# Weight sums of the seven-for-eight groups by accumulating DMAs instead of VectorE subtractions

## The chip, the cores and the metric

The kernel runs on one core of one Trainium2 chip. The metric is the device time of one execution in microseconds. Before the change it is 3290.38 us, the median of three runs between 3289.5 and 3291.68 us.

## The reference, cut to what matters

The reference is one layer of one model followed by one layer of another, on 256 tokens of width 2048, all in float32. The first layer mixes tokens with a state space branch and a gated delta rule, then has a feed-forward network with a convolution. The second layer has a feed-forward network, a pooling and linear attention mixer, and a second feed-forward network. The change touches only the two feed-forward networks of the second layer:

```python
def swiglu(h, w_in, w_out):          # h: 256 x 2048, D_FF = 5632
    gu = h @ w_in                    # w_in: 2048 x 11264
    gate, up = gu[..., :D_FF], gu[..., D_FF:]
    return (jax.nn.silu(gate) * up) @ w_out

h = h + 0.5 * swiglu(rmsnorm_2(h, ffn1_norm[l]), ffn1_w_in[l], ffn1_w_out[l])
...
h = h + 0.5 * swiglu(rmsnorm_2(h, ffn2_norm[l]), ffn2_w_in[l], ffn2_w_out[l])
```

## The kernel before

Float32 products are made of three reduced-precision products. Each operand is split into a high part (a cast to fp32r) and a low part (the rest). For a weight block of 128x1024, loaded as 512 KB, ScalarE makes the high part (line 126) and VectorE subtracts it to get the low part (line 127), in `split_raw`. TensorE then adds high x high, high x low and low x high into PSUM.

The main stream of a feed-forward network runs through `gemm_tg` (lines 201 to 203): each block feeds 12 matmuls of 512 columns. Its blocks are loaded by `load_w` (line 85) on SP's queue into four `wr` buffers; the high and low parts have three buffers each (`wh`, `wl`).

The 5632 hidden columns are worked in 11 groups of 512, each with a gate half and an up half. Six groups are `plain`. The groups 3, 4, 5, 7 and 9 are made by `seven`. It treats the product as a 2x2 block problem: the 256 tokens are two halves of 128, the 2048 inputs are two halves of 1024, and gate and up are the two halves of the outputs. With sums of activations (made once in `x_sums`, kept in `sx`) and sums of weight blocks it needs seven block products where the plain way needs eight. Each `seven` call has 28 passes: a pass takes one weight block or one weight sum of 128x1024, splits it into `sh` and `sl` (two buffers each) and runs 6 matmuls (lines 1133 to 1135) into one of four PSUM banks `ps[0]` to `ps[3]`.

`together` interleaves the two streams: one step is one pass of `seven` and one block of the main stream (up blocks of a `plain` group or blocks of the down projection `down_g`), so 6 and 12 matmuls. The tile framework sets the order of instructions on each engine from the order in the code and their priority; splits and weight sums are raised with `tc.high_priority(offset=600)`. Semaphores are put in by the framework where a tile is written, read or its buffer reused.

In `seven` before the change, `block` loads a weight block with SP: the first of each chain through `load_w`, the others into three `ws` buffers (line 1142). `less` makes a weight sum as a VectorE subtraction (recorded at the helper's line 368) into one of two `tt` buffers. In the first loop the sums form a chain for each of four `jj`: t1 = b12 - b11, t2 = b22 - t1, t4 = b21 - t2, and the four passes of one `jj` follow each other. In the second loop each `jj` has three passes, one of them on the sum b22 - b12. At the end of a group the banks are added to partial results kept in `w5`, `w6` and `gs`, and gate and up are joined.

Of the kernel before, what the change touches and what calls it, by code (L numbers as in the profile page):

```python
# [11 lines left out]
F32 = mybir.dt.float32  # L12
# [3 lines left out]
ALU = mybir.AluOpType  # L16
PSUM = bass.MemoryType.PSUM

P = 128
# [32 lines left out]
def tile_kernel(ctx: ExitStack, tc: tile.TileContext, A, out):  # L52
    nc = tc.nc
    act, dve, pe, pool_e, sp = nc.scalar, nc.vector, nc.tensor, nc.gpsimd, nc.sync
# [11 lines left out]
    def bank():  # L66
        if side_full[0]:
            return pg.tile([P, 512], F32, tag="pt", name="side2")
        return px.tile([P, 512], F32, tag="side", name="side")

    def v3(ap, b):
        return ap.rearrange("p (a b) -> p a b", b=b)
# [10 lines left out]
    def load_w(src, n=1024):  # L83
        raw = wp.tile([P, n], F32, tag="wr", bufs=4, name="wr")
        sp.dma_start(out=raw, in_=src)
        return raw

    x0, xq0 = [], []
    for q in range(4):
        t = xp.tile([P, 4, T], F32, tag=f"x{q}", name=f"x{q}")  # L90
# [207 lines left out]
    class Norm:  # L298
# [5 lines left out]
        def add(self, q, t, xk):  # L304
            if self.ss is None:
                self.ss = ev2.tile([P, 4, 2], F32, tag="ss", bufs=3, name="ss")
            junk = ev2.tile([P, 512], F32, tag="sq", bufs=1, name="sq")
            act.activation(junk, xk, AF.Square, accum_out=self.ss[:, q, t : t + 1])
            if (q, t) == (2, 1):
                act.activation(warm, self.ss[:, 2, :], AF.Sqrt)  # L310
# [56 lines left out]
    def sub(o, a, b):  # L367
        dve.tensor_tensor(out=o, in0=a, in1=b, op=ALU.subtract)  # L368
# [7 lines left out]
    def stt(o, a, s, b, op0, op1):  # L376
        dve.scalar_tensor_tensor(out=o, in0=a, scalar=s, in1=b, op0=op0, op1=op1)
# [43 lines left out]
    def wsrc(name, b, n=2):  # L421
        return [A[name][n * b + i] for i in range(n)]
# [6 lines left out]
    ps = bank()  # L429
# [11 lines left out]
    first = [gemm_f32(raw0 if b == 0 else [load_w(s) for s in wsrc("w_u", b)], xg) for b in range(nu)]  # L441
# [239 lines left out]
    for hd in range(HEADS):  # L681
        t = mp.tile([P, 2, T], F32, tag=f"qk{hd}", name=f"qk{hd}")
        v = mp.tile([P, T], F32, tag=f"v{hd}", name=f"v{hd}")
        for part, dst in ((0, t[:, 1, :]), (1, t[:, 0, :]), (2, v)):
            b = 3 * hd + part
            if b % 6 == 5:
                ps = gemm_f32([load_w(s) for s in wsrc("w_qkv", b)], x0)
            else:
                ps = gemm(wsrc("w_qkv", b), hs)
# [5 lines left out]
    raw = wp.tile([P, KT * 16], F32, tag="wr", bufs=4, name="wba")  # L695
# [5 lines left out]
    ps = pg.tile([P, T], F32, tag="pt", name="pt")  # L701
# [63 lines left out]
    for m in range(8):  # L765
        ps = gemm(wsrc("w_z", m), hs)
# [248 lines left out]
    for q in range(4):  # L1015
        t = xp.tile([P, 2, 512], F32, tag=f"x{q}", name=f"xt{q}")
# [33 lines left out]
    def ffn(up, down, hs, rstd, conv_w, scale, fin, gain=None, nxt=None, before_last=None):  # L1050
        with tc.tile_pool(name="hid", bufs=2) as hd:
# [48 lines left out]

            sx = []

            def x_sums():
                for j in range(8):
                    f = hd.tile([P, 2, T], F32, tag="g", bufs=1, name="xf")
                    s = hd.tile([P, 4, P], F32, tag="w", bufs=1, name="xs")
                    for i in range(2):
                        add(f[:, i, :], hs[j + 8 * i][:, 0, :].bitcast(F32), hs[j + 8 * i][:, 1, :].bitcast(F32))  # L1110
                    add(s[:, 0, :], f[:, 0, P:], f[:, 1, P:])
                    sub(s[:, 1, :], s[:, 0, :], f[:, 0, :P])
                    sub(s[:, 2, :], f[:, 0, :P], f[:, 0, P:])
                    sub(s[:, 3, :], f[:, 1, :P], s[:, 1, :])
                    e = []
                    for i in range(2):
                        t = hp.tile([P, 2, 2, P], F32R, tag=f"h{j + 8 * i}", name=f"sx{j}_{i}")
                        act.copy(out=t[:, 0], in_=s[:, 2 * i : 2 * i + 2, :])
                        sub(t[:, 1], s[:, 2 * i : 2 * i + 2, :], t[:, 0].bitcast(F32))
                        e += [(t[:, 0, c, :], t[:, 1, c, :]) for c in range(2)]  # L1120
                    sx.append(e)
                    yield

            def seven(g):

                ps = [px.tile([P, 512], F32, tag="side", name="side7") for _ in range(4)]

                def passes(ps, xa, raw, first, last):
                    to = [hd.tile([P, 1024], F32R, tag=n, bufs=2, name=n) for n in ("sh", "sl")]
                    hi, lo = (v3(a, 512) for a in split_raw(raw, to=to))  # L1130
                    for i in range(2):
                        xh, xl = xa(i)
                        pe.matmul(ps, xh, hi[:, i, :], start=first and i == 0, stop=False, skip_group_check=True)  # L1133
                        pe.matmul(ps, xh, lo[:, i, :], start=False, stop=False, skip_group_check=True)  # L1134
                        pe.matmul(ps, xl, hi[:, i, :], start=False, stop=last and i == 1, skip_group_check=True)  # L1135

                def block(k2, half, tag=None):
                    src = A[up][16 * g + 8 * half + k2]
                    if tag is None:
                        return load_w(src)  # L1140
                    raw = hd.tile([P, 1024], F32, tag=tag, bufs=3, name="ws")
                    sp.dma_start(out=raw, in_=src)
                    return raw

                def less(a, b):
                    t = hd.tile([P, 1024], F32, tag="tt", bufs=2, name="tt")
                    with tc.high_priority(offset=600):
                        sub(t, a, b)
                    return t

                def hx(k, t):
                    return lambda i: (hs[k + i][:, 0, P * t : P * t + P], hs[k + i][:, 1, P * t : P * t + P])

                def sxs(j, c):
                    return lambda i: sx[j + i][c]

                gs, w5, w6 = (hd.tile([P, 512], F32, tag=n, bufs=1, name=n) for n in ("g", "w", "w6"))
                for jj in range(4):
                    j, fl = 2 * jj, dict(first=jj == 0, last=jj == 3)
                    b11, b12 = block(jj, 0), block(jj, 1, "ws")  # L1160
                    t1 = less(b12, b11)
                    passes(ps[0], hx(j, 0), b11, **fl)
                    if jj == 3:
                        act.copy(out=w6, in_=ps[0])
                    yield
                    b22 = block(4 + jj, 1, "ws")
                    passes(ps[1], sxs(j, 0), t1, **fl)
                    if jj == 3:
                        add(w5, ps[1], w6)
                    yield  # L1170
                    b21 = block(4 + jj, 0, "ws")
                    t2 = less(b22, t1)
                    passes(ps[2], sxs(j, 1), t2, **fl)
                    if jj == 3:
                        add(gs, ps[2], w6)
                    yield
                    t4 = less(b21, t2)
                    passes(ps[3], hx(8 + j, 1), t4, **fl)
                    if jj == 3:
                        add(w6, ps[3], w6)  # L1180
                    yield
                for jj in range(4):
                    j, fl = 2 * jj, dict(first=False, last=jj == 3)
                    passes(ps[0], hx(8 + j, 0), block(4 + jj, 0, "ws"), **fl)
                    yield
                    b22 = block(4 + jj, 1, "ws")
                    passes(ps[1], sxs(j, 3), b22, **fl)
                    yield
                    passes(ps[2], sxs(j, 2), less(b22, block(jj, 1, "ws")), **fl)
                    yield  # L1190
                rc = late[0]
                t = hd.tile([P, 2, 512], F32, tag="tt", bufs=2, name="gates")
                act.activation(t[:, 0], ps[0], AF.Silu, scale=rc[:, 0:1])
                add(t[:, 1], ps[2], w6)
                act.activation(t[:, 1], t[:, 1], AF.Silu, scale=rc[:, 1:2])
                add(gs, ps[1], gs)
                add(w5, ps[2], w5)
                a = gs, w5
                for i in range(2):
                    stt(a[i], a[i], rc[:, i : i + 1], t[:, i], ALU.mult, ALU.mult)  # L1200
                yield
                new_ys(g)
                return_turn = lambda: turn_hidden(a, ys[g])
                if g == 3:
                    pend.append(return_turn)
                else:
                    after.append(return_turn)
                yield
# [108 lines left out]
    half = cst2[:, P + 5 * T : P + 5 * T + 2]  # L1317
# [162 lines left out]
    for g in range(4):  # L1480
        up = gp_.tile([P, 2, 16 + T], F32, tag="up", bufs=2, name="up")
# [202 lines left out]
```

## Time and profile before

| what | value |
|---|---|
| median of three runs | 3290.38 us |
| the profiled execution, whole program | 3289.64 us |
| its span | 3287.8 us |
| TensorE clock granted in it | 0.999 of full speed |
| busy share: PE, VectorE, ScalarE, GpSimd | 99%, 79%, 54%, 0% |
| read from HBM | 661 MB |

The span is the time from the first to the last instruction of the profiled execution; what the program takes beyond it lies around it. PE is TensorE's matmul side and PEld its weight loads, which overlap. DVE is VectorE, ACT ScalarE, POOL GpSimd, and SP the engine whose queue issues the loads (SPq). L1133 is line 1133 of the kernel. A group of instructions is named by what it writes and reads, `sl<-tt,sh` being the low part of a weight sum. A wait is put down to what released it.

### The profile page before, as it was taken

How to read it: one execution, taken by the hardware profiler on the slowest of the kernel's cores; microseconds unless marked ns; L12 is line 12 of the kernel's file. 1: busy time of each engine (PE TensorE's matmuls, PEld its weight loads, DVE VectorE, ACT ScalarE, POOL GpSimd, SP SyncE). 2: the span in 40 equal slices, each digit the busy share in tenths (PEclk: the TensorE clock that was granted, in tenths of full speed). 3: DMA queues.
4: the chain of work that ended last, by engine and by line, in shares of the span. 5: the costliest groups of instructions: out<-in, count | busy, mean ns of one | idle time of the engine just before them, and what ended most of it. 6: DMA issues, size and time to landing. Idle time of an engine off the chain costs nothing.

```text
span 3287.8 us, 44587 instructions
## 1 busy us (share of the span) xinstructions
PE 3265.2 (99%) x16530; PEld 2742.9 (83%) x16530; DVE 2588.5 (79%) x3758; ACT 1774.7 (54%) x2523; POOL 4.0 (0%) x22
## 2 busy tenths in 40 slices
PE   9999999999999999999999999999999999999998
PEld 8887988888888888888888888888888888888887
DVE  8999987666877767677987887875786988878876
ACT  4566666445555445455655555545555655555554
POOL 0000000000000000000000000000000000000000
PEclk9999999999999999999999999999999999999999
DMA  6445543365555555556777777765545677777774
GB/s 223 156 152 174 179 144 116 108 225 180 192 187 188 190 188 188 188 187 204 255 247 248 246 247 243 246 197 190 173 146 195 229 243 248 249 245 243 247 253 148
DMA packets 186873, 666.09 MB, mean 203 GB/s; under 512 B 20880, under 2 KB 25488, under 8 KB 186272
## 3 DMA queue, kind: packets, MB, share of 16 engines
q1 hardware_dynamic: 186080, 662.21, 61.3%
q8 instruction: 129, 2.11, 0.3%
q10 hardware_dynamic: 576, 1.05, 0.1%
q14 instruction: 88, 0.72, 0.1%
HBM read 661.08 MB, written 2.10 MB: 202 GB/s over the span
## 4 chain that ended last, share of the span: by engine, by line
PE 94%; DVE 4%; issue 1%; ACT 1%; DMA 0%; SPq 0%; DVEq 0%
PE ptt L201 18%; PE ptt L202 18%; PE ptt L203 18%; PE pt L170 13%; PE pt L172 6%; PE side L1134 4%; PE side L1135 4%; PE side L1133 4%; DVE wl L127 1%; PE pt L135 1%; PE pt L137 1%; PE pt L136 1%; PE pt L245 1%; PE side L874 1%; PE side L885 1%; PE side L620 1%
## 5 line engine op out<-in xcount | busy, mean ns | idle before, releaser
L126 ACT CAST wh<-wr 128x1024 fp32r<-128x1024 f32 x937 | 984.2, 1051 | 1221.9 <-PE ptt L203 839.4
L127 DVE TENSOR_TENSOR wl<-wr,wh 128x1024 fp32r<-128x1024 f32 x937 | 1146.1, 1223 | 539.0 <-ACT wh L126 534.2
L170 PE MATMUL pt<-h,wh 128*128 128x512 f32 x1792 | 632.1, 397 | 0.0
L172 PE MATMUL pt<-h,wl 128*128 128x256 f32 x1792 | 502.5, 281 | 0.0
L201 PE MATMUL ptt<-wh,h 128*128 128x512 f32 x1088 | 428.3, 394 | 0.0
L202 PE MATMUL ptt<-wl,h 128*128 128x512 f32 x1088 | 425.5, 391 | 0.0
L203 PE MATMUL ptt<-wh,h 128*128 128x512 f32 x1088 | 424.2, 390 | 0.0
L202 PE MATMUL ptt<-wl,hid 128*128 128x512 f32 x1040 | 409.0, 394 | 0.0
L201 PE MATMUL ptt<-wh,hid 128*128 128x512 f32 x1040 | 408.4, 393 | 0.5 <-ACT wh L126 0.5
L203 PE MATMUL ptt<-wh,hid 128*128 128x512 f32 x1040 | 408.4, 394 | 0.0
L170 PEld LDWEIGHTS pt<-h,wh 128*128 128x128 f32 x1792 | 336.3, 188 | 80.9 <-issue 1.0
L172 PEld LDWEIGHTS pt<-h,wl 128*128 128x128 f32 x1792 | 338.3, 189 | 0.6
L201 PEld LDWEIGHTS ptt<-wh,h 128*128 128x128 f32 x1088 | 204.2, 188 | 46.7 <-ACT wh L126 1.2
L203 PEld LDWEIGHTS ptt<-wh,h 128*128 128x128 f32 x1088 | 204.3, 188 | 44.0 <-issue 0.4
L202 PEld LDWEIGHTS ptt<-wl,h 128*128 128x128 f32 x1088 | 204.2, 188 | 43.4
L201 PEld LDWEIGHTS ptt<-wh,hid 128*128 128x128 f32 x1040 | 195.4, 188 | 45.7 <-ACT wh L126 1.0
L202 PEld LDWEIGHTS ptt<-wl,hid 128*128 128x128 f32 x1040 | 195.6, 188 | 44.1
L203 PEld LDWEIGHTS ptt<-wh,hid 128*128 128x128 f32 x1040 | 195.4, 188 | 43.6 <-DVE hid L368 0.5
L127 DVE TENSOR_TENSOR sl<-tt,sh 128x1024 fp32r<-128x1024 f32 x160 | 195.9, 1224 | 21.9 <-ACT sh L126 21.3
L126 ACT CAST sh<-tt 128x1024 fp32r<-128x1024 f32 x160 | 168.3, 1052 | 52.9 <-PE side L1135 48.1
L135 PE MATMUL pt<-h,wl 128*128 128x256 f32 x512 | 149.5, 292 | 0.0
L137 PE MATMUL pt<-h,wh 128*128 128x256 f32 x512 | 145.3, 284 | 0.0
(420 smaller groups left out, 4957.9 us busy)
## 6 DMA issues: line engine op xcount, KB each, us to landing
wr<-in_f_up SPq DMA_DIRECT2D x408, 512.0 KB, 4.3
wr<-in_f_down SPq DMA_DIRECT2D x265, 512.0 KB, 4.3
ws<-in_f_up SPq DMA_DIRECT2D x240, 512.0 KB, 4.3
wr<-in_w_qkv SPq DMA_DIRECT2D x48, 512.0 KB, 3.3
wr<-in_w_gs SPq DMA_DIRECT2D x32, 512.0 KB, 3.3
wr<-in_w_gd SPq DMA_DIRECT2D x32, 512.0 KB, 3.3
wr<-in_w_glu SPq DMA_DIRECT2D x32, 512.0 KB, 3.3
wr<-in_w_out SPq DMA_DIRECT2D x32, 512.0 KB, 3.3
```

The lines of the kernel that those rows point to most:

```text
L126: act.copy(out=hi, in_=raw)
L127: dve.tensor_tensor(out=lo, in0=raw, in1=hi.bitcast(F32), op=ALU.subtract)
L135: pe.matmul(ps, wl, xt[:, 0, :], start=first, stop=False)
L137: pe.matmul(ps, wh, xt[:, 0, :], start=False, stop=last)
L170: pe.matmul(ps.rearrange("p a b -> p (a b)"), hi[:, j, :], xts[k].rearrange("p a b -> p (a b)"), start=k == 0, stop=False, skip_group_chec ...
L172: pe.matmul(ps[:, 0, :], lo[:, j, :], xts[k][:, 0, :], start=False, stop=k == n - 1, skip_group_check=True)
L201: pe.matmul(pss[t], xh, hi[:, j, :], start=k == 0, stop=False)
L202: pe.matmul(pss[t], xh, lo[:, j, :], start=False, stop=False)
L203: pe.matmul(pss[t], xl, hi[:, j, :], start=False, stop=k == n - 1)
L1133: pe.matmul(ps, xh, hi[:, i, :], start=first and i == 0, stop=False, skip_group_check=True)
L1134: pe.matmul(ps, xh, lo[:, i, :], start=False, stop=False, skip_group_check=True)
L1135: pe.matmul(ps, xl, hi[:, i, :], start=False, stop=last and i == 1, skip_group_check=True)
```

## The change

In `seven` a weight sum is no longer subtracted on VectorE. The first block of a chain is loaded by SP into one of now five `tt` tiles (`base`); after a pass has split that tile, a DMA issued by GpSimd adds the next block onto it in place (`accum_op=ALU.add`), and the next pass of the chain splits the same tile again. Two chains (`pair`) alternate. [...] `block`, `less` and the three `ws` buffers are gone; one block in the second loop is loaded by `load_w`.

```diff
-                    add(s[:, 0, :], f[:, 0, P:], f[:, 1, P:])
-                    sub(s[:, 1, :], s[:, 0, :], f[:, 0, :P])
+                    sub(s[:, 0, :], f[:, 1, P:], f[:, 0, P:])
+                    stt(s[:, 1, :], s[:, 0, :], -1.0, f[:, 0, :P], ALU.mult, ALU.subtract)
                     sub(s[:, 2, :], f[:, 0, :P], f[:, 0, P:])
-                    sub(s[:, 3, :], f[:, 1, :P], s[:, 1, :])
+                    stt(s[:, 3, :], f[:, 1, :P], -1.0, s[:, 1, :], ALU.mult, ALU.subtract)
...
+                def src(k2, half):
+                    return A[up][16 * g + 8 * half + k2]
+
+                def base(k2, half):
+                    t = hd.tile([P, 1024], F32, tag="tt", bufs=5, name="tt")
+                    sp.dma_start(out=t, in_=src(k2, half))
                     return t
...
-                for jj in range(4):
-                    j, fl = 2 * jj, dict(first=jj == 0, last=jj == 3)
-                    b11, b12 = block(jj, 0), block(jj, 1, "ws")
-                    t1 = less(b12, b11)
-                    passes(ps[0], hx(j, 0), b11, **fl)
...
-                    b22 = block(4 + jj, 1, "ws")
-                    passes(ps[1], sxs(j, 0), t1, **fl)
...
-                    b21 = block(4 + jj, 0, "ws")
-                    t2 = less(b22, t1)
-                    passes(ps[2], sxs(j, 1), t2, **fl)
...
-                    t4 = less(b21, t2)
-                    passes(ps[3], hx(8 + j, 1), t4, **fl)
...
+                for pair in ((0, 1), (2, 3)):
+                    tt = {jj: base(jj, 0) for jj in pair}
+                    for n in range(4):
+                        for jj in pair:
+                            xa = (hx(2 * jj, 0), sxs(2 * jj, 0), sxs(2 * jj, 1), hx(8 + 2 * jj, 1))[n]
+                            passes(ps[n], xa, tt[jj], first=jj == 0, last=jj == 3)
+                            if n < 3:
+                                pool_e.dma_start(out=tt[jj], in_=(src(jj, 1), src(4 + jj, 1), src(4 + jj, 0))[n],
+                                                 accum_op=ALU.add)
...
+                            yield
+                for pair in ((0, 1), (2, 3)):
+                    tt = {jj: base(4 + jj, 1) for jj in pair}
+                    for n in (1, 2, 0):
+                        for jj in pair:
+                            xa = (hx(8 + 2 * jj, 0), sxs(2 * jj, 3), sxs(2 * jj, 2))[n]
+                            passes(ps[n], xa, tt[jj] if n else load_w(src(4 + jj, 0)), first=False, last=jj == 3)
+                            if n == 1:
+                                pool_e.dma_start(out=tt[jj], in_=src(jj, 1), accum_op=ALU.add)
+                            yield
...
-                add(gs, ps[1], gs)
-                add(w5, ps[2], w5)
+                stt(gs, gs, -1.0, ps[1], ALU.mult, ALU.subtract)
+                stt(w5, w5, -1.0, ps[2], ALU.mult, ALU.subtract)
```

## Rows read from the trace of the kernel before

**Rows 1.** The page's head and first line of part 1: busy us (share) xinstructions.
```profile
span 3287.8 us, 44587 instructions
...
PE 3265.2 (99%) x16530; PEld 2742.9 (83%) x16530; DVE 2588.5 (79%) x3758; ACT 1774.7 (54%) x2523; POOL 4.0 (0%) x22
```

**Rows 2.** The page's part 4, shares of the chain by engine.
```profile
PE 94%; DVE 4%; issue 1%; ACT 1%; DMA 0%; SPq 0%; DVEq 0%
```

**Rows 3.** Windows: start:end length, busy us (x) per engine, PEclk, DMA share, GB/s.
```profile
1577.70:2213.00 635.30, 635.30 (x2796) 517.62 (x2795) 525.27 (x527) 338.36 (x351) 0.00 (x0) 1.00 0.74 241
2612.00:3213.00 601.00, 601.00 (x2646) 489.68 (x2645) 493.50 (x466) 318.22 (x326) 0.00 (x0) 1.00 0.76 246
```

**Rows 4.** Longest waits of PE, whole run: total us, times, longest us.
```profile
PE side L438 <- DVE sq L365: 6.2, 1, 6.2
PE side L655 <- DVE xa L362: 5.4, 4, 3.6
```

**Rows 5.** Tile `tt`: xcount, ns min/median/max, first and last start in us.
```profile
L368 DVE TENSOR_TENSOR tt<-ws,tt x80: 1217/1225/1236, 1573.3 to 3157.0; 128x1024 f32<-128x1024 f32 x80
L368 DVE TENSOR_TENSOR tt<-ws,wr x40: 1215/1225/1243, 1567.6 to 3144.6; 128x1024 f32<-128x1024 f32 x40
L368 DVE TENSOR_TENSOR tt<-ws x40: 1217/1226/1227, 1634.0 to 3204.3; 128x1024 f32<-128x1024 f32 x40
```

**Rows 6.** Tile `gates`, VectorE at a group's end.
```profile
L365 DVE TENSOR_TENSOR gates<-side,w x10: 683/684/687, 1694.0 to 3223.1; 128x512 f32<-128x512 f32 x10
...
L377 DVE SCALAR_TENSOR_TENSOR g<-g,rc,gates x10: 744/751/754, 1696.4 to 3219.7; 128x512 f32<-128x512 f32 x10
```

**Rows 7.** Longest wait of GpSimd, whole run.
```profile
POOL mean_g L1319 <- PE ptt L203: 2256.9, 1, 2256.9
```

**Rows 8.** Waits of SP's queue, 1569 to 2200 us.
```profile
SPq L1142 <- DVE tt L368: 138.9, 74, 3.2
```

**Rows 9.** DMA issues, 1569 to 2215 us: xcount, KB each, median us to landing.
```profile
ws<-in_f_up SPq DMA_DIRECT2D x117, 512.0 KB, 4.3
wr<-in_f_up SPq DMA_DIRECT2D x101, 512.0 KB, 4.5
```

**Rows 10.** Timeline around 1802 us: start, length in us, instruction [idle before <-releaser].
```profile
1802.84 0.39 PE L1133 MATMUL side<-sh,sx 128*128 128x512 f32 x1
...
1804.44 1.05 ACT L126 CAST sh<-ws 128x1024 fp32r<-128x1024 f32 x1 [0.35 <-PE side L1135]
...
1805.52 1.23 DVE L127 TENSOR_TENSOR sl<-ws,sh 128x1024 fp32r<-128x1024 f32 x1 [0.18 <-ACT sh L126]
...
1811.19 0.39 PE L1133 MATMUL side<-sh,sx 128*128 128x512 f32 x1
```

**Rows 11.** DMA issues, 600 to 800 us.
```profile
wr<-in_w_out SPq DMA_DIRECT2D x32, 512.0 KB, 3.3
...
gb<-in_gain SPq DMA_DIRECT2D x1, 1024.0 KB, 5.5
```

**Rows 12.** DMA packets and issues, 2590 to 2612 us.
```profile
DMA packets 1751, 6.37 MB, mean 290 GB/s; under 512 B 199, under 2 KB 199, under 8 KB 1750
...
wr<-in_f_up SPq DMA_DIRECT2D x9, 512.0 KB, 5.5
ws<-in_f_up SPq DMA_DIRECT2D x5, 512.0 KB, 5.3
```

**Rows 13.** Timeline of PE in a plain stage, first and last of 15 starts.
```profile
2547.79 0.39 PE L203 MATMUL ptt<-wh,yg 128*128 128x512 f32 x1
...
2550.97 0.39 PE L202 MATMUL ptt<-wl,yg 128*128 128x512 f32 x1
```

**Rows 14.** Tile `side`, the first matmul line of a pass.
```profile
L1133 PE MATMUL side<-sh,sx x320: 393/394/483, 1581.9 to 3221.4; 128*128 128x512 f32 x160
...
L1133 PE MATMUL side<-sh,h x240: 393/394/483, 1577.7 to 3213.0; 128*128 128x512 f32 x120
```

More of the change, by code (lines that the diff above doesn't have):

```diff
@@ L1135, in passes @@
                         pe.matmul(ps, xl, hi[:, i, :], start=False, stop=last and i == 1, skip_group_check=True)
[L1137 to L1148, printed above, removed]
+                def src(k2, half):
[3 more added lines that the diff above has]
+                    sp.dma_start(out=t, in_=src(k2, half))
                     return t
@@ L1157, in seven @@
                 gs, w5, w6 = (hd.tile([P, 512], F32, tag=n, bufs=1, name=n) for n in ("g", "w", "w6"))
-                for jj in range(4):
-                    j, fl = 2 * jj, dict(first=jj == 0, last=jj == 3)
-                    b11, b12 = block(jj, 0), block(jj, 1, "ws")
-                    t1 = less(b12, b11)
-                    passes(ps[0], hx(j, 0), b11, **fl)
-                    if jj == 3:
-                        act.copy(out=w6, in_=ps[0])
-                    yield
-                    b22 = block(4 + jj, 1, "ws")
-                    passes(ps[1], sxs(j, 0), t1, **fl)
-                    if jj == 3:
-                        add(w5, ps[1], w6)
-                    yield
-                    b21 = block(4 + jj, 0, "ws")
-                    t2 = less(b22, t1)
-                    passes(ps[2], sxs(j, 1), t2, **fl)
-                    if jj == 3:
-                        add(gs, ps[2], w6)
-                    yield
-                    t4 = less(b21, t2)
-                    passes(ps[3], hx(8 + j, 1), t4, **fl)
-                    if jj == 3:
-                        add(w6, ps[3], w6)
-                    yield
@@ L1182, in seven @@
[L1182 to L1190, printed above, removed]
+                for pair in ((0, 1), (2, 3)):
[7 more added lines that the diff above has]
+                                                 accum_op=ALU.add)
+                            if jj == 3 and n == 0:
+                                act.copy(out=w6, in_=ps[0])
+                            elif jj == 3:
+                                add((w5, gs, w6)[n - 1], ps[n], w6)
+                            yield
@@ L1191, in seven @@
                 rc = late[0]
-                t = hd.tile([P, 2, 512], F32, tag="tt", bufs=2, name="gates")
+                t = hd.tile([P, 2, 512], F32, tag="tt", bufs=5, name="gates")
                 act.activation(t[:, 0], ps[0], AF.Silu, scale=rc[:, 0:1])
```

## The prediction

> **What bounds the kernel now.** I read the page's head and part 1 first: the span is 3287.8 us and TensorE is busy for 99% of it [rows 1]. The program's own time in that execution was 3289.64 us, 1.84 us more than the span; the median of the three timed runs is 3290.38 us, 0.7 us above it, so sums made against this execution hold for the median to within 1 us. The profile says that a busy PE need not be at its peak, so the chain of waits came next: it is PE for 94% [rows 2]. Then the windows: the change touches only the two stretches in which seven-for-eight groups run, about 1577 to 2213 us and 2612 to 3213 us, 1236 us together. PE is busy in every microsecond of them, VectorE 82 to 83%, ScalarE 53%, GpSimd not at all, and the DMA engines are taken for 74 to 76% at 241 to 246 GB/s [rows 3]. Last the waits of PE: over the whole run its largest two are 6.2 and 5.4 us, both at lines 438 and 655 of the first stages; no line of `seven` is among them [rows 4]. So PE, fed without a gap, bounds these stretches, and VectorE's 82% costs nothing now. Work taken off VectorE can't shorten them by itself; the change can only keep PE fed or starve it.
>
> **The change, part by part.**
>
> *Subtractions taken off VectorE.* `less` makes 160 weight sums (80 + 40 + 40) of 1.225 us [rows 5]: 196 us of VectorE go, all beside PE work. Gain: 0. Were the cover gone (VectorE late), they would be worth something, but PE has no wait on VectorE here [rows 4].
>
> *Small edits.* In `x_sums` a sum becomes a difference and two differences become multiply-subtracts, same count and size. At a group's end two additions become multiply-subtracts: 0.684 against 0.751 us at 128x512 [rows 6], 2 x 0.067 x 10 groups = 1.3 us of VectorE beside PE. Cost: 0. The order of the passes changes (two interleaved chains), their number does not: 28 passes of 6 matmuls in each of 10 groups, so PE's work is the same. The tiles take the same room (three plus two before, five after).
>
> *Loads moved.* The bytes read from HBM stay: 28 blocks of 512 KB per group. Of these, 16 per group, 160 in all, leave SP's queue for GpSimd's, which issues nothing in these stretches (its one long wait is 2256.9 us [rows 7]). SP loses a blocking wait: 138.9 us of its time in the first stretch were spent on a buffer that a subtraction had to free [rows 8]. So the main stream's loads are issued no later than now; gain 0, since PE does not wait for them. In the last third of a group two direct loads now follow each other in the four `wr` buffers of the main stream, which leaves it about two steps of lead instead of three; with landings of 4.3 to 4.5 us [rows 9] against 8.3 us for two steps that holds.
>
> *The new chain.* This is where time can be lost. Today a sum needs two loaded blocks and a VectorE subtraction. Afterwards the tile of a chain must go through: ScalarE cast, VectorE subtraction of the low half (both read the tile), then the accumulating DMA may start, then it must land, and only then can the cast for the next pass of that chain begin. Two chains alternate, so a chain has two steps for a round. From the timeline [rows 10]: passes two apart begin at 1802.84 and 1811.19, so two steps are 8.35 us. The cast for the later pass starts at 1804.44 and its low half is done at 1805.52 + 1.23 = 1806.75: 2.31 us of work, finished 4.44 us ahead of need. The hand-overs that the rows show are 0.18 us (ScalarE to VectorE) and 0.35 us (PE to ScalarE); I take 0.5 us for the two new ones. So a chain keeps pace for ever if an accumulating DMA lands within 8.35 - 2.31 - 0.5 = 5.54 us of its issue, and over the three accumulations of a chain the 4.44 us of lead pay for 1.48 us more each: the limit is 7.0 us. Beyond it PE stands still for 3 x (landing - 7.0) at the end of each pair of chains; both chains are late together, so this counts once per pair. There are 2 such pairs in a group's first loop, 20 in all: 60 us for each microsecond over 7.0. The second loop has one accumulation per chain and would need 5.54 + 4.44 = 10 us to stall. Behind a late tile the cast waits on ScalarE, and behind it the cast of the main stream; that one is about two steps ahead of its use, so PE meets the late pass first.
>
> *How long an accumulating DMA takes.* No row shows one. Below, it is a plain load in these stretches, 4.3 to 4.5 us [rows 9]. Above, nearest rows: it reads the block and the tile, 1024 KB through the same engines, and in an uncrowded stretch a 1024 KB load lands in 5.5 us where one of 512 KB needs 3.3 [rows 11], so 2.2 us more. With today's 4.4 us that is 6.6 us. But the queues get fuller: in the first loop a step asks for two blocks and three quarters of a second read, 2.75 x 0.524 MB in 4.175 us = 346 GB/s counted so, against 246 now; in the fullest stretch of this trace, at 290 GB/s, plain loads land in 5.3 to 5.5 us [rows 12], which with 2.2 gives 7.6 us. What GpSimd takes to issue one has no row; SP's 0.33 us is in the rows' landings, and I add nothing. Far ends: 4.3 us (a plain load, the second read free) and three such loads in turn (read, read, write), 13 us. I take 7.25 us, between 6.6 and 7.6 and nearer to the fuller stretch, because loop one asks for more than that stretch did. Sum: 0.25 x 3 x 20 = +15 us; 3289.6 + 15 = 3304.6, say 3305 us.
>
> The Trainium skill, in Collectives: The Full Stack, section "The bandwidth ceiling", says that a reduction in the DMA engines runs at half the rate of a copy because it reads two sources, measured as 32.35 against 62.28 GB/s over two engines; as an estimate from that page 512 KB on 16 engines take 2.0 us against 1.05, only 1 us more. By that, 5.4 + 1.0 = 6.4 us would stay under the limit and the sum would be 3290 us; no row here shows an accumulating transfer.
>
> **The rivals.**
>
> *Chains keep up (same time).* If accumulating DMAs land within 7.0 us, nothing is late and all that goes and comes is hidden: 3290 us, within 6 us. For it: 6.6 us by today's landings, and a 4.44 us lead that each pair gets anew. Against: the fuller queues. This is the nearest rival.
>
> *PE's own rhythm (faster).* Place: the matmuls of these stretches. In a step 36 starts take 8.35 us, 0.232 us each [rows 10]; in a plain stage 14 starts take 50.97 - 47.79 = 3.18 us, 0.227 us each [rows 13]. The rows name no wait for the difference. There are 560 line-1133 matmuls, so 280 steps of 18 [rows 14]: 5040 x 0.0048 = 24 us lie there. If a lighter VectorE or other timing of the casts lets half of them fall into the short rhythm, the time is 3278 us; it decides from a third on (-8 us). Against: the plain stage has busy VectorE too, so its load hardly sets the rhythm. It could also go the other way.
>
> *DMA engines saturate (much slower).* If they can't carry the 346 GB/s counted above but only the 290 seen for 22 us [rows 12], a step of the first loop takes 2.75 x 0.524 / 0.290 = 4.97 us instead of 4.175, over 160 steps: +127 us, 3417 us. Against: that stretch got what it asked for; its ceiling is not shown.
>
> *GpSimd held while VectorE works (slower).* If issuing had to wait for a running VectorE subtraction, up to 1.23 us [rows 10] come on top: 8.5 us, +90 us, 3380 us. The Trainium skill (SBUF — State Buffer, "Who interferes with whom") says that a VectorE instruction with two SBUF inputs contends with GpSimd instructions that read SBUF, but takes it, by inference, that descriptor generation only writes; by that page this case is unlikely, and no row shows it.
>
> **How the numbers follow.** Chains somewhat late (landing 7.1 to 7.9 us, +6 to +54 us): 0.38, its own range 3296 to 3344. Chains keep up: 0.37. PE's rhythm falls: 0.14. Saturation 0.07, GpSimd held 0.04. A difference of 0.2%, 6.6 us, is about what a measurement of this kernel can tell from none. Faster 0.14; same 0.37; slower 0.38 + 0.11 = 0.49. Range 3281 to 3345: it holds the first two cases and most of the third, and leaves out some 0.05 below and 0.13 above.
>
> **What would show it.** `less` gone and VectorE near 66 to 67% in these stretches: first step. GpSimd issuing 160 DMAs and their landing time: the term that decides; under 7.0 us with no PE wait on the casts of `sh` or the halves `sl`: the chains keep up. PE waits on `sh` or `sl`, 20 clusters of a microsecond or so, always towards the third accumulation of a pair: the forecast. Waits spread over all steps and plain loads landing past 7 us: saturation. GpSimd's issues lasting as long as a VectorE instruction: the last rival. A time under 3283 us with PE starts nearer to 0.227 us: the rhythm. The prediction is wrong if the time moves while no wait on `sh` or `sl` appears.

## The result and the profile after

The changed kernel takes 3348.99 us (median of four runs, 3338.57 to 3354.36) against 3291.03 us of the kernel before in the same runs: a ratio of 1.0171, with a 95% interval of 1.0159 to 1.0184. The direction was forecast, the size was not: +58 us instead of +15, and 4 us above the range. The profiled execution took 3345.80 us with a span of 3344.0 us, so 56 us more than that of before.

The page of the changed kernel: span, engines, chain by engine, and the two large DMA queues (packets, MB, share of 16 engines).

```profile
span 3344.0 us, 44515 instructions
...
PE 3286.9 (98%) x16530; PEld 2742.4 (82%) x16530; DVE 2389.5 (71%) x3598; ACT 1755.7 (53%) x2523; POOL 142.3 (4%) x182
...
q1 hardware_dynamic: 163040, 578.31, 51.1%
q0 software_dynamic: 23040, 83.90, 14.5%
...
PE 74%; DMA 11%; DVE 7%; issue 5%; ACT 2%; POOL 0%; SPq 0%; ACTq 0%; POOLq 0%; DVEq 0%
```

PE did the same 16530 matmuls, but it stood idle for 3344.0 - 3286.9 = 57 us where it had 23 before [rows 1]. The other 22 us of the difference lie in matmuls that are shown longer, such as those of 0.50 and 0.51 us in the rows below, against 0.39 us in [rows 10]. VectorE lost 199 us. The chain of waits, 94% PE before [rows 2], now runs through DMA for 11% of the span.

The windows of the two stretches (their ends are shifted, since they are longer), in the columns of [rows 3], and two windows of 100 us inside:

```profile
1577.70:2255.00 677.30, 659.25 (x2858) 528.12 (x2857) 435.11 (x452) 334.38 (x358) 67.32 (x78) 1.00 0.83 228
2660.00:3265.00 605.00, 589.77 (x2553) 472.53 (x2552) 382.16 (x373) 297.93 (x314) 63.88 (x74) 0.99 0.84 233
...
2700.00:2800.00 100.00, 96.73 (x416) 77.49 (x416) 62.81 (x62) 47.31 (x50) 8.63 (x10) 0.98 0.84 233
2800.00:2900.00 100.00, 96.67 (x412) 77.08 (x410) 64.57 (x64) 47.97 (x49) 9.18 (x11) 0.98 0.82 227
```

PE is no longer busy all the time in them, VectorE has fallen to 63 to 64%, and the DMA engines are taken for 83 to 84% while they move fewer bytes per second than before. Who PE waits for, first of the matmuls, then of the weight loads, and what the casts of ScalarE wait for (total us, times, longest):

```profile
PE side L1135 <- DVE sl L127: 18.9, 30, 0.8
PE side L1134 <- ACT sh L126: 13.1, 18, 1.4
```
```profile
PEld side L1135 <- DVE sl L127: 35.2, 47, 1.1
PEld side L1134 <- ACT sh L126: 20.9, 19, 1.9
```
```profile
ACT sh L126 <- DMA tt<-in_f_up: 368.7, 140, 7.5
```

The trace of before has no wait of PE on `sh` or `sl` at all; [rows 4] shows its two longest waits. The casts of the weight sums wait for the accumulating DMA, the low halves for the casts, and PE for both. The DMA issues tell how long a landing takes, first from 1569 to 2240 us, beside [rows 9], then the accumulating ones of the whole run:

```profile
wr<-in_f_up SPq DMA_DIRECT2D x102, 512.0 KB, 5.8
tt<-in_f_up POOLq DMA_DIRECT2D x78, 512.0 KB, 7.6
wr<-in_f_down SPq DMA_DIRECT2D x78, 512.0 KB, 4.7
tt<-in_f_up SPq DMA_DIRECT2D x35, 512.0 KB, 6.0
```
```profile
tt<-in_f_up POOLq DMA_DIRECT2D x160, 512.0 KB, 7.5
```

The plain loads beside them land later as well, in 4.7 to 6.0 us where [rows 9] has 4.3 to 4.5.

One pair of chains in the timeline of GpSimd, its six issues in the order first chain, second chain, and then the cast that waited for the first of them:

```profile
1703.30 0.86 POOL L1160 DMA_DIRECT2D tt<-in_f_up  x1 [28.16 <-DVE sl L127]
1704.43 0.86 POOL L1160 DMA_DIRECT2D tt<-in_f_up  x1 [0.27 <-DVE sl L127]
1716.11 0.86 POOL L1160 DMA_DIRECT2D tt<-in_f_up  x1 [10.81 <-DVE sl L127]
1719.94 0.86 POOL L1160 DMA_DIRECT2D tt<-in_f_up  x1 [2.97 <-DVE sl L127]
1724.75 0.86 POOL L1160 DMA_DIRECT2D tt<-in_f_up  x1 [3.95 <-DVE sl L127]
1731.49 0.86 POOL L1160 DMA_DIRECT2D tt<-in_f_up  x1 [5.88 <-DMA wr<-in_f_up]
```
```profile
1713.51 1.05 ACT L126 CAST sh<-tt 128x1024 fp32r<-128x1024 f32 x1 [7.51 <-DMA tt<-in_f_up]
1714.59 1.22 DVE L127 TENSOR_TENSOR sl<-tt,sh 128x1024 fp32r<-128x1024 f32 x1 [7.33 <-ACT sh L126]
1714.61 0.51 PE L1134 MATMUL side<-sh,sx 128*128 128x512 f32 x1 [0.53 <-ACT sh L126]
...
1715.87 0.50 PE L1135 MATMUL side<-sl,sx 128*128 128x512 f32 x1 [0.75 <-DVE sl L127]
```

The first two DMAs go out 1.13 us apart and land, by the view of line 1160 in these two moments, 10.1 and 12.8 us later:

```profile
DMA to landing us min/median/max: 10.1/10.1/10.1
```
```profile
DMA to landing us min/median/max: 12.8/12.8/12.8
```

The cast of the first chain starts at 1713.51, its matmul 1.1 us behind, and PE already waits at the first accumulation: whatever lead this pair had is gone with it.

### The profile page after: what moved, and what is told of

It is laid out like the page before. It is cut to its first block, busy times and chain, and to the rows that moved or that the text cites. A ratio compares the mean times of both kernels' runs of the same rounds, so it can differ in the third digit from the quotient of the medians.

```text
span 3344.0 us, 44515 instructions
## 1 busy us (share of the span) xinstructions
PE 3286.9 (98%) x16530; PEld 2742.4 (82%) x16530; DVE 2389.5 (71%) x3598; ACT 1755.7 (53%) x2523; POOL 142.3 (4%) x182
## 3 DMA queue, kind: packets, MB, share of 16 engines
q0 software_dynamic: 23040, 83.90, 14.5%
## 4 chain that ended last, share of the span: by engine, by line
PE 74%; DMA 11%; DVE 7%; issue 5%; ACT 2%; POOL 0%; SPq 0%; ACTq 0%; POOLq 0%; DVEq 0%
PE ptt L203 13%; PE ptt L201 13%; PE ptt L202 13%; PE pt L170 13%; DMA tt<-in_f_up 10%; PE pt L172 6%; PE side L1135 2%; PE side L1136 2%; PE side L1134 2%; DVE wl L127 2%; DVE sl L127 2%; ACT sh L126 1%; PE pt L135 1%; PE pt L137 1%; PE pt L136 1%
## 5 line engine op out<-in xcount | busy, mean ns | idle before, releaser
L127 DVE TENSOR_TENSOR sl<-tt,sh 128x1024 fp32r<-128x1024 f32 x240 | 293.0, 1223 | 329.5 <-ACT sh L126 328.3
L126 ACT CAST sh<-tt 128x1024 fp32r<-128x1024 f32 x240 | 251.8, 1050 | 412.3 <-DMA tt<-in_f_up 368.7
L1160 POOL DMA_DIRECT2D tt<-in_f_up x120 | 103.7, 864 | 2534.0 <-DVE sl L127 2353.4
```

Of the source, the lines that this page charges most:

```text
L126: act.copy(out=hi, in_=raw)
L127: dve.tensor_tensor(out=lo, in0=raw, in1=hi.bitcast(F32), op=ALU.subtract)
L1160: pool_e.dma_start(out=tt[jj], in_=(src(jj, 1), src(4 + jj, 1), src(4 + jj, 0))[n], accum_op=ALU.add)
```

## The experiments

Theory A is the prediction's: a chain waits for its own accumulating DMA, and PE stands still when the landing passes what the round of a chain allows. Rivals were named with each run. All of them are edits of the changed kernel; times are medians, with the ratio to the kernel before in the same runs.

**Four chains.** The pairs of both loops become one set of four.

```diff
-                for pair in ((0, 1), (2, 3)):
+                for pair in ((0, 1, 2, 3),):
```

> Four chains of tiles alternate instead of two; the same transfers, adds and passes. Theory A (each chain waits for its own accumulating DMA): a chain now has four steps, 16.7 us, for a round in place of 8.35, so a DMA may land as late as about 13 us after its issue and no wait on sh or sl is left: 3285 to 3297 us. Rival B (the second read fills the DMA engines): the same bytes and reads are asked for in the same time, so most of the added time stays: 3330 us or more.

3290.77 us against 3290.65 us, ratio 1.0002 (0.9993 to 1.0011). The windows and the DMA issues:

```profile
1577.70:2213.00 635.30, 635.30 (x2794) 517.63 (x2793) 433.47 (x441) 337.45 (x351) 67.33 (x78) 1.00 0.85 239
2612.00:3213.00 601.00, 601.00 (x2646) 489.76 (x2645) 405.17 (x388) 318.34 (x326) 66.44 (x77) 1.00 0.87 244
```
```profile
tt<-in_f_up POOLq DMA_DIRECT2D x160, 512.0 KB, 7.8
```

The landings are no shorter, 7.8 us, and the DMA engines are even fuller, 85 to 87%; yet PE is busy in every microsecond again. So the time was not lost to full engines (rival B) but to the wait of each chain for itself: no wait of PE on `sh` or `sl` is left in this trace.

**One chain at a time.**

```diff
-                for pair in ((0, 1), (2, 3)):
+                for pair in ((0,), (1,), (2,), (3,)):
```

> One chain after another, so a chain has one step, 4.2 us, for a round. Theory A: with landings of 5.5 to 7.7 us each accumulation of the first loop is 4.1 to 6.3 us late, three per chain less 4.4 us of lead, four chains in ten groups: 320 to 660 us more than before, 3610 to 3950 us, and VectorE and the DMA engines less busy. Rival B (full DMA engines): traffic is no higher, so about the time of the changed kernel, 3349 us, or a little less.

3762.49 us (one run), in the middle of what theory A gave. PE's longest wait, the landing and the stretch:

```profile
PE side L1134 <- ACT sh L126: 270.0, 132, 5.7
```
```profile
tt<-in_f_up POOLq DMA_DIRECT2D x160, 512.0 KB, 5.8
```
```profile
1577.70:3600.00 2022.30, 1736.50 (x7222) 1361.65 (x7220) 1081.66 (x1270) 829.82 (x1003) 132.70 (x163) 0.94 0.63 177
```

Landings are shorter here and the engines emptier (63%), and the kernel is 472 us slower than before: the number of chains decides, not the traffic. That the time hit the middle is partly luck: by theory A's arithmetic a landing of 5.8 us gives some 350 us, and the granted clock of 0.94 over 2022 us can hold an estimated 120 us of the rest at most.

**Plain transfers in place.**

```diff
-                                pool_e.dma_start(out=tt[jj], in_=(src(jj, 1), src(4 + jj, 1), src(4 + jj, 0))[n],
-                                                 accum_op=ALU.add)
+                                pool_e.dma_start(out=tt[jj], in_=(src(jj, 1), src(4 + jj, 1), src(4 + jj, 0))[n])
...
-                                pool_e.dma_start(out=tt[jj], in_=src(jj, 1), accum_op=ALU.add)
+                                pool_e.dma_start(out=tt[jj], in_=src(jj, 1))
```

> The DMAs of GpSimd's queue overwrite the tile instead of adding to it (the weight sums are left out); queue, waits and chains stay. Theory A with the second read as its cause: a landing falls to that of a plain load, 4.5 to 5.7 us, under the limit of 7.0, and the waits go: 3286 to 3297 us. Rival C (GpSimd's queue itself is slow, added or not): landings stay over 7 us and the time over 3330 us. Rival B gives 3290 us as well.

3290.91 us against 3290.65 us, ratio 1.0001 (0.9992 to 1.0011). The issues, and the queue of GpSimd:

```profile
tt<-in_f_up POOLq DMA_DIRECT2D x160, 512.0 KB, 4.5
```
```profile
q0 software_dynamic: 23040, 83.90, 7.7%
```

Through the same queue, with the same waits, a plain transfer lands in 4.5 us. So neither the queue nor the way it is issued is slow; the addition is. The same 83.90 MB take 7.7% of the engines' span here and 14.5% in the changed kernel: with the spans, 253 and 485 us, a factor of 1.9.

**VectorE's additions in the new order.** `more` loads the block by SP into one of two `ws` buffers and adds it in place; `tt` gets three buffers to make room.

```diff
-                                pool_e.dma_start(out=tt[jj], in_=(src(jj, 1), src(4 + jj, 1), src(4 + jj, 0))[n],
-                                                 accum_op=ALU.add)
+                                more(tt[jj], (src(jj, 1), src(4 + jj, 1), src(4 + jj, 0))[n])
...
-                                pool_e.dma_start(out=tt[jj], in_=src(jj, 1), accum_op=ALU.add)
+                                more(tt[jj], src(jj, 1))
```

> The changed order of passes, the two chains and the turned signs stay, but each next block is loaded by SP into one of two buffers and added by VectorE in place, 160 additions. Theory A: nothing of the order costs anything, 3286 to 3298 us with VectorE back at some 82% of these stretches. Rival D (the order of the passes or the small edits cost the time): 3330 us or more.

3289.10 us against 3290.65 us, ratio 0.9996 (0.9987 to 1.0005). Order, chains and the negated sums cost nothing. (Each step of a chain now adds where it subtracted; that is why some activation sums and partial results are negated in the diff.)

**Smaller accumulations.** Two kernels, with 768 and with 512 of the 1024 columns added (here the first).

```diff
-                                pool_e.dma_start(out=tt[jj], in_=(src(jj, 1), src(4 + jj, 1), src(4 + jj, 0))[n],
+                                pool_e.dma_start(out=tt[jj][:, :768], in_=(src(jj, 1), src(4 + jj, 1), src(4 + jj, 0))[n][:, :768],
                                                  accum_op=ALU.add)
...
-                                pool_e.dma_start(out=tt[jj], in_=src(jj, 1), accum_op=ALU.add)
+                                pool_e.dma_start(out=tt[jj][:, :768], in_=src(jj, 1)[:, :768], accum_op=ALU.add)
```

> As the changed kernel, but every accumulating DMA adds only 768 of the 1024 columns (a quarter of each weight sum is left out). Theory A: a landing is shorter by the service of a quarter, 8 packets x 0.082 us for its own and as much again where loads alternate with it, so 6.3 to 6.9 us instead of 7.6, at the limit of 7.0; what is left are the slowest of them: 3292 to 3310 us. Rival E (each accumulating DMA costs a fixed 57 / 160 = 0.36 us, by issue or hand-over, whatever its size): 3340 to 3352 us.

> The same with 512 of the 1024 columns (half of each weight sum is left out). Theory A: landings of 5.2 to 6.0 us, under the limit: 3286 to 3296 us. Rival E: 3340 to 3352 us.

3294.67 us with 768 columns, ratio 1.0009 (1.0000 to 1.0019), and 3291.54 us with 512, ratio 1.0000 (0.9991 to 1.0010). Their landings:

```profile
tt<-in_f_up POOLq DMA_DIRECT2D x160, 384.0 KB, 5.9
```
```profile
tt<-in_f_up POOLq DMA_DIRECT2D x160, 256.0 KB, 4.6
```

The number of accumulating DMAs is the same as in the changed kernel, so a price per DMA (rival E) is refuted. At a median of 5.9 us the slowest few still cost some 3 us, at the edge of what the interval tells from nothing; at 4.6 us nothing. The first landed in less time than I expected (6.3 to 6.9 us).

**Half of the main stream's loads.**

```diff
-        for s in srcs:
-            hi, lo = (v3(a, 512) for a in split_w(s))
+        for m, s in enumerate(srcs):
+            if not side_full[0] or m % 2 == 0:
+                raw = load_w(s)
+            hi, lo = (v3(a, 512) for a in split_raw(raw))
```

> As the changed kernel with full accumulating DMAs, but while seven-for-eight groups run the main stream loads only every second of its blocks and uses it twice (half of its weights are left out). Theory A with competition: the 328 ns packets of the accumulating DMAs no longer alternate with as many plain ones, landings fall from 7.6 to 6.0 to 6.8 us and the time to 3288 to 3305 us. If the landing is long by itself or because two accumulating DMAs share GpSimd's one queue, it stays over 7.2 us and the time over 3325 us.

3293.58 us against 3291.57 us, ratio 1.0006 (0.9997 to 1.0016).

```profile
tt<-in_f_up POOLq DMA_DIRECT2D x160, 512.0 KB, 5.4
```

With fewer plain loads beside them, full accumulating DMAs land in 5.4 us instead of 7.5, below what I expected, and the waits are all but gone. So competition with the plain loads is a good part of the landing.

**Accumulating DMAs in the second loop alone.** The kernel with VectorE's additions, with the second loop's four DMAs put back:

```diff
-                                more(tt[jj], src(jj, 1))
+                                pool_e.dma_start(out=tt[jj], in_=src(jj, 1), accum_op=ALU.add)
```

> Accumulating DMAs only in the second loop, one per chain (40 in all); the 120 sums of the first loop are loads by SP and additions on VectorE. Theory A: one accumulation per chain may land 10 us after its issue before PE waits, so 3287 to 3296 us. Rival E: 40 x 0.36 = 14 us more, 3305 us.

3292.44 us against 3291.57 us, ratio 1.0001 (0.9992 to 1.0010).

```profile
tt<-in_f_up POOLq DMA_DIRECT2D x40, 512.0 KB, 7.2
```

With landings of 7.2 us, over the limit of the first loop, the second loop costs nothing: its chains accumulate once and have the whole lead for it.

**One of the two chains by DMA.** In the first loop only odd `jj` accumulate by DMA; the rest adds on VectorE.

```diff
-                                pool_e.dma_start(out=tt[jj], in_=(src(jj, 1), src(4 + jj, 1), src(4 + jj, 0))[n],
-                                                 accum_op=ALU.add)
+                                nxt_ = (src(jj, 1), src(4 + jj, 1), src(4 + jj, 0))[n]
+                                if jj % 2:
+                                    pool_e.dma_start(out=tt[jj], in_=nxt_, accum_op=ALU.add)
+                                else:
+                                    more(tt[jj], nxt_)
...
-                                pool_e.dma_start(out=tt[jj], in_=src(jj, 1), accum_op=ALU.add)
+                                more(tt[jj], src(jj, 1))
```

> Of each pair in the first loop only the second chain gets its sums by accumulating DMAs (60 in all); the first chain and the second loop add on VectorE. Theory A with the partner as what made the second chain's landings long (8.2 us on the mean of a pair's second chain, 7.2 on its first): alone in GpSimd's queue the second chain's DMAs land within 6.0 to 6.9 us and the time is 3287 to 3297 us. If plain loads alone make them long, they still land in 7.5 us or more and the second chain is as late as before: 3320 us or more.

3291.48 us against 3291.64 us, ratio 1.0001 (0.9991 to 1.0011).

```profile
tt<-in_f_up POOLq DMA_DIRECT2D x60, 512.0 KB, 5.7
```

Without a partner the second chain's DMAs land in 5.7 us (mean 6.0). So the partner is the other part of the landing. Whether it delays the second chain's DMA in GpSimd's queue or on the engines, no run separates.

No version beats the kernel before: where PE is never kept waiting, the time is the same within 0.1%, whether VectorE has 82% or 68% to do. Turning further plain groups into seven-for-eight groups with VectorE's free time was not tried.

## Why the prediction was wrong

**Right: what bounds the kernel.** VectorE's 196 us bring nothing (e1: 68% busy, same time), and the small edits and the order cost nothing (e4). The new chain is what costs, and PE waits on `sh` and `sl`. On the average the limit of 7.0 us for two chains sorts the versions rightly: those with medians from 4.5 to 5.9 us lose 0 to 3 us, the one with 7.5 us loses 58. The step "the second loop has one accumulation per chain" holds (e8).

**Wrong: the landing, 7.25 us for both chains alike.** This is the main term of the sum that was mis-sized. The two chains are not alike. Over the 120 issues of line 1160, taken in turn, those of the first chain of a pair land in 7.24 us on the mean, just what I took, but those of the second in 8.16 us; the first accumulation of a pair alone in 8.4 and 9.9 us. I made one landing time of it and wrote that both chains are late together. PE waits for the later one: 3 x (8.16 - 7.0) x 20 = 70 us by the prediction's own formula, where 56 were measured; what that leaves over is the next step. What made the second longer is the first: two accumulating DMAs go out within a step, at the start of a pair 1.13 us apart, while SP loads on, and each takes the engines for 1.9 times as long as a plain one. I had added the second read to one DMA's landing, but not the partner's in front of it (e9: 5.7 us alone). The slope, 60 us for each microsecond, turns the 0.9 us that were missing into 55: with such a slope the range should have reached to a landing of 8.2 us.

**Wrong too: 4.44 us of lead for every pair.** The limit of 7.0 us rests on it, and it was read from one pass in the middle of a stretch [rows 10]. Matmul by matmul against the kernel with plain transfers (e3), whose order is the same, 54 us of the loss fall into 13 of the 20 pairs, 1.8 to 6.2 us each; seven pairs lose nothing. Here are the pair shown above and one of the seven: their windows, in the columns of [rows 3], the landings of the six DMAs of each, and where the first pass of each begins:

```profile
1703.30:1742.20 38.90, 35.44 (x154) 27.48 (x153) 20.08 (x19) 18.28 (x21) 5.18 (x6) 1.00 0.89 240
1968.70:2007.90 39.20, 39.20 (x176) 32.06 (x175) 23.65 (x23) 19.61 (x22) 5.16 (x6) 1.00 0.93 267
```
```profile
DMA to landing us min/median/max: 5.7/8.0/12.8
DMA to landing us min/median/max: 5.7/8.0/10.8
```
```profile
1704.76 0.39 PE L1134 MATMUL side<-sh,h 128*128 128x512 f32 x1
...
1968.69 0.86 POOL L1160 DMA_DIRECT2D tt<-in_f_up  x1 [28.20 <-DVE sl L127]
...
1975.84 0.39 PE L1134 MATMUL side<-sh,h 128*128 128x512 f32 x1
```

Both pairs have a median landing of 8.0 us, yet PE waits only in the first. There its first pass begins 1.5 us after the first DMA went out, in the other 7.2 us after. Counted as the prediction did, from the end of the low half to the pass, the first chain's lead is 1.8 to 4.2 us in the 13 pairs that lose and 5.3 us or more in the seven that don't. The prediction's formula with each pair's own leads and landings gives 52 us, with 4.44 us for all 69; for 768 columns and for half of the main loads it gives 3.7 and 1.5 us, where 3.1 and 2.0 were measured. So the sign that was named, 20 clusters at the third accumulation, failed as well: fewer pairs wait, and in the pair above PE waits from the first accumulation on. With plain transfers, where nothing is late, four pairs have a lead of 1.8 us too; what sets it is open.

A smaller part comes from the clock. In three windows of 100 us, two of them shown above, the granted clock is 0.98 on the mean; 2% of 300 us is 6 us at most. Before, no such window stood in these stretches [rows 3].

**Half the rate.** The Trainium skill (Collectives: The Full Stack, "The bandwidth ceiling") gives the half rate for reductions between cores. The trace agrees for an accumulation onto a tile: 1.9 times the engines' time for the same bytes (e3). The 6.4 us that I worked out from it missed what the rows show: it adds the engine time of one transfer's own second read, and here the transfer lies beside plain loads and a partner (e7, e9). For a lone chain, with 5.7 to 5.8 us (e9, e2), it would have been on the long side.

**The rivals.** Chains that keep up: no, but four chains do (e1). Saturation: refuted by e1, whose engines carry the same traffic at 85 to 87% without a wait (the 346 GB/s of its sum are 345). GpSimd held by VectorE: each issue took 0.86 us (862 ns at least and in the median of 160, 1005 ns at most), beside VectorE busy for 63 to 64%; nothing held it for as long as an instruction of VectorE, which is what the Trainium skill (SBUF — State Buffer, "Who interferes with whom") infers. PE's rhythm: no version got faster by it; where it comes from stays open.

## What to carry to other kernels

When work moves from an engine to an accumulating DMA, its price, here, is no longer busy time but the round of a dependent chain: read, land, read again. Count the steps between two touches of the same tile, compare them with the landing under the kernel's own load and with all chains in flight, and add chains until the round is longer; here two cost 58 us and four nothing. Read the lead at the start of each chain, not at one place: here it was 1.8 us in some pairs and 7 us in others, and the short ones paid. And work that is taken off an engine that nobody waits for brought no time, 196 us of it.

## What the runs showed of the hardware

GpSimd issued an accumulating DMA of 512 KB in 0.86 us and a plain one in 0.53 us (e3), while SP takes 0.33 us for one of its own before the change. In the kernel with one chain, where PE stood still again and again, the granted clock was 0.94 on the mean over 2022 us: between its two levels of 2.4 and 1.2 GHz that is an estimated 11 to 13% of the time at the lower one. In the kernel with four chains, which kept PE busy, it was 1.00.
